# Row maximum over 16384 rows: other load sizes, and other shares of two engines

## The chip, the core and the metric

One core of a Trainium2 chip runs the kernel. The metric is the device time of one execution in microseconds; the median of several runs is compared. Engines: VectorE (DVE) does elementwise work and reductions along a partition's row; ScalarE (ACT) copies; TensorE (PE) transposes here; GpSimd (POOL) can reduce across partitions; SyncE (SP) issues the loads, which 16 DMA engines carry out.

## The reference

```python
def setup_inputs():
    batch, seq, dim = 32, 512, 1024
    return {"x": np.random.randn(batch, seq, dim).astype(np.float32)}

def reference(x):
    return np.max(x, axis=-1).astype(np.float32)
```

So 16384 rows of 1024 numbers, 67.11 MB, are read from memory, and each row gives its maximum.

## The kernel before

**Layout.** The 16384 rows are spread over 128 partitions, 128 rows to each. They come in two blocks of rows: 112 rows a partition, and 16. In each block a partition's rows lie one behind the other in memory, so a load of n rows moves n x 4096 contiguous bytes for each of the 128 partitions. `BLOCKS` lists n for every load, in order. Two rows of the last block are not in the list: they come last, cut at columns 532 and 592 into four `pieces` (`PIECES`), so that little work is left behind the last bytes.

**The ring.** All loads go into `ring`, a buffer of 47 rows a partition behind the results. A load takes the next rows of the ring, or starts again at row 0 if it doesn't fit before its end. `issue()` sends every load as soon as, in the order of the plan, all readers of the rows that it overwrites have been written down; the wait itself is a semaphore on SP. SP issues all loads on one queue in order, so a load that waits holds back all behind it.

**The work on a load.** Load j has n rows. `SHARED[j] = (m, parts)` says that of m of its rows the first `parts` blocks of 128 columns go another way than DVE; the other rows, and what is left of the m, go to DVE. The steps:

- `dj` (direct): DVE takes the maximum of each of the n-m whole rows, one reduce instruction (L78).
- `tk` (turn): for chunk k, at most 8 blocks, PE transposes each block of 128 x 128 into the PSUM tile `ps` (L160), ACT copies this into `sb` (L166), and POOL takes the maximum over all partitions (L168) into `top`. After the transposition the partitions are the columns. `ps`, `sb` and `top` have two buffers each.
- `bk` (back): PE turns each 128 results of chunk k, which lie in one partition's row, into a column (L178), of `got` or of `joint`.
- `pj` (partial): DVE reduces the remaining columns of the m rows to one or more numbers beside these columns, in the same tile.
- `mj` (merge): DVE takes the maximum over blocks and remaining columns of the m rows. Loads named in `RANK` have no merge of their own: their columns stand in one tile, `joint`, and one merge `m99` at the very end takes all of them.
- `fq` (final): DVE reduces one of the four pieces. f2 and f3 take the first result in with them, which stands in the column before their piece.

Before, four loads are shared: three rows of load 10 in full (24 blocks), two rows of loads 13 and 14 by three blocks (6 and 6), and one row of load 17 by two blocks: 38 blocks of 128 columns.

**The order.** `PLAN` is a list of these steps written out by hand, and it is the order of the instructions: `in_turn` ties each instruction to the one ahead of it on the same engine. So every engine works through its instructions in the order of the list, and one that waits for a semaphore holds all behind it. What waits for what follows from the tiles: a reader of a tile waits for its writer, and a writer of a tile or a buffer for those that used it before. Results leave by two stores of ACT: the first block's behind f0, the second block's behind m99.

Of the kernel before, what the change touches and what calls it, by code (L numbers as in the profile page):

```python
# [8 lines left out]
F32 = mybir.dt.float32  # L9

BLOCKS = [
    [2, 15, 16, 14, 11, 11, 10, 10, 8, 8, 7],
    [3, 3, 3, 2, 1, 1, 1],
]
RING = 47


SHARED = {10: (3, 8), 13: (2, 3), 14: (2, 3), 17: (1, 2)}  # L20

RANK = {13: 1, 14: 2, 17: 2}

PIECES = [(532, 492), (592, 432)]

PLAN = """
    d0 d1 d2 d3 d4 d5 d6 d7 d8 d9 t0 d10 t1 t2 d11 b0 d12 b1 d13 t3 p13 b2 p14 t4 m10 d15 b3
    d16 p17 t5 f0 b4 f1 f2 b5 f3 m99
""".split()

NOSYNC = mybir.DependencyInfo(mybir.DependencyClass.NoSync, mybir.DependencyReason.DATA)
# [4 lines left out]
def kernel(  # L41
# [35 lines left out]
    def maximum(out, in_):  # L77
        return in_turn("DVE", nc.vector.reduce_max(out=out, in_=in_, axis=X))  # L78
# [20 lines left out]
    for sizes in BLOCKS:  # L99
# [7 lines left out]
        b, place = 0, {}  # L107
        for i in sorted(range(len(sizes)), key=lambda i: RANK.get(base + i, 0)):
            place[i] = b
# [8 lines left out]
    assert first == I  # L118
    shared = [SHARED.get(j, (0, C)) for j in range(len(loads))]

    lead = [0 if RANK.get(j) == 3 else n - m for j, ((_, n, _, _), (m, _)) in enumerate(zip(loads, shared))]
    final = [j for j in range(len(loads)) if j in RANK]
    final.sort(key=lambda j: loads[j][3])
# [11 lines left out]
    def rows(j):  # L135
        start, n, _, _ = loads[j]
        return ring[:, I + start * D:I + (start + n) * D].rearrange("p (i d) -> p i d", d=D)
# [4 lines left out]
    def share(j):  # L142
        m, parts = shared[j]
        if j in RANK:
            r = loads[j][3] + lead[j] - col0
            return joint[:, r:r + m, :]
        if j not in fetched:
            got = psmall.tile([P, m, parts + (parts < C)], F32)
            fetched[j] = got
        return fetched[j]  # L150
# [39 lines left out]
    def partial(j):  # L190
        m, parts = shared[j]

        s = width - parts if j in RANK else 1
        maximum(share(j)[:, :, parts:], rows(j)[:, lead[j]:lead[j] + m, parts * P:].rearrange(
# [102 lines left out]
```

## Time and profile before

| | |
|---|---|
| median of 3 runs | 163.82 us (163.78 to 163.9) |
| span of the profiled execution | 162.1 us |
| DVE busy | 135.3 us, 83% of the span, 33 instructions |
| POOL busy | 15.9 us, 10 instructions |
| PE busy | 13.6 us, 76 matmuls |
| ACT busy | 6.3 us, 7 instructions |
| moved by DMA | 67.18 MB, mean 414 GB/s |
| mean granted TensorE clock | 0.955 |

The profiled execution has a span of 162.1 us, from its first to its last instruction; the time of a run is taken around that and is 1.7 us longer.

How to read the profile: the span is cut into 40 slices, and a digit is the busy share of an engine in its slice, in tenths. A group of instructions is one line of the code with one form; it shows how often it ran, its busy time, the mean length of one in ns, and the time for which the engine stood idle ahead of it with what ended that. The chain of work that ended last is followed back from the end: at each step to what released the instruction, or to the instruction before it on its engine. In the timeline a line shows start, length, engine, line, operation, and tiles, out<-in; in brackets stands how long the engine was idle, and what released it. For a load, the time from issue to landing is shown. Line numbers are those of the kernel before; in the kernel after they are two less.

### The profile page before, as it was taken

What the parts mean: (1) busy time and instruction counts of PE and PEld (TensorE: products, weight loads), DVE (VectorE), ACT (ScalarE), POOL (GpSimd) and SP (SyncE); (2) the same over time, 40 slices, a digit from 0 to 9 for tenths busy, and PEclk for the clock granted to TensorE, in tenths of its full rate; (3) what the DMA queues carried; (4) which work ended last, traced back from release to release, by engine and by line L of the source; (5) the groups of instructions that cost most, each with busy time, mean ns of one, the idle gap of its engine ahead of it and who ended that gap; (6) DMA issues with size and microseconds to landing.
All of it is one profiled execution on the core that took longest, in us unless ns stands there. A gap on an engine that the chain in (4) does not pass through costs nothing.

```text
span 162.1 us, 295 instructions
## 1 busy us (share of the span) xinstructions
PE 13.6 (8%) x76; PEld 11.7 (7%) x76; DVE 135.3 (83%) x33; ACT 6.3 (4%) x7; POOL 15.9 (10%) x10
## 2 busy tenths in 40 slices
PE   0000000000000000000000000000000000772942
PEld 0000000000000000000000000000000000762731
DVE  3500019998399999999999999996999999999994
ACT  3000000000000000000000000000000000241120
POOL 0000000000000000000000000000000000099791
PEclk9999999999999999999999999999999999996555
DMA  5995999599879999898999799799999989999991
GB/s 178 566 485 258 470 501 517 259 517 517 354 340 439 453 404 534 356 523 367 478 411 475 334 485 475 334 485 388 477 429 388 466 382 446 415 421 416 411 388 34
DMA packets 3456, 67.18 MB, mean 414 GB/s; under 512 B 640, under 2 KB 896, under 8 KB 1536
## 3 DMA queue, kind: packets, MB, share of 16 engines
q1 hardware_dynamic: 3168, 67.11, 96.8%
q10 hardware_dynamic: 288, 0.07, 0.2%
HBM read 67.11 MB, written 0.07 MB: 414 GB/s over the span
## 4 chain that ended last, share of the span: by engine, by line
DMA 50%; DVE 47%; SPq 1%; issue 0%; DVEq 0%
DMA ring<-in_x_dram 50%; DVE ring L78 45%; DVE joint L78 2%; SPq L238 1%; DVEq L292 0%
## 5 line engine op out<-in xcount | busy, mean ns | idle before, releaser
L78 DVE TENSOR_REDUCE ring<-ring 128x1 f32<-128x1024 f32 (+13 forms) x20 | 129.9, 6547 | 23.5 <-DMA ring<-in_x_dram 23.5
L168 POOL PARTITION_ALL_REDUCE top<-sb x6 | 15.7, 2658 | 142.6 <-ACT sb L166 142.5
L160 PE MATMUL ps<-ident,ring 128*128 128x128 f32 x38 | 9.0, 423 | 140.0 <-DMA ring<-in_x_dram 140.0
L160 PEld LDWEIGHTS ps<-ident,ring 128*128 128x128 f32 x38 | 7.6, 225 | 140.1 <-issue 140.1
L166 ACT COPY sb<-ps 128x1024 f32<-128x1024 f32 (+2 forms) x6 | 5.0, 834 | 150.5 <-PE ps L160 143.5
L78 DVE TENSOR_REDUCE joint<-ring 128x2 f32<-128x1280 f32 (+1 forms) x3 | 3.9, 1314 | 0.0
L178 PE MATMUL got<-ident,top 1*128 1x1 f32 x24 | 2.7, 228 | 3.8 <-POOL top L168 3.6
L178 PEld LDWEIGHTS got<-ident,top 1*128 1x128 f32 x24 | 2.4, 188 | 4.6 <-POOL top L168 4.6
L178 PE MATMUL joint<-ident,top 1*128 1x1 f32 x14 | 2.0, 244 | 1.9 <-POOL top L168 1.9
L178 PEld LDWEIGHTS joint<-ident,top 1*128 1x128 f32 x14 | 1.7, 210 | 2.7 <-POOL top L168 2.7
L166 ACT ACT_TABLE_LOAD x1 | 1.3, 1283 | 0.7 <-PEq L281 0.7
L83 DVE MEMSET ident<- 128x128 f32 x1 | 0.2, 165 | 0.8 <-PEq L281 0.8
L90 DVE TENSOR_SCALAR rowno<-rowno 32x1 f32<-32x1 f32 x3 | 0.4, 146 | 0.1
L85 DVE TENSOR_TENSOR_SCAN colno<-ident 128x128 f32<-128x128 f32 x1 | 0.4, 425 | 0.0
L92 DVE TENSOR_SCALAR ident<-colno,rowno 128x128 f32<-128x128 f32 x1 | 0.3, 288 | 0.0
L87 DVE STREAM_TRANSPOSE rowno<-colno 128x32 f32<-128x32 f32 x1 | 0.2, 211 | 0.0
L78 DVE TENSOR_REDUCE ring<-got 128x3 f32<-128x24 f32 x1 | 0.2, 172 | 0.0
L78 DVE TENSOR_REDUCE ring<-joint 128x5 f32<-128x20 f32 x1 | 0.2, 170 | 0.0
L281 POOL MEMSET const-float32-0.0<- 128x1 f32 x1 | 0.1, 98 | 0.2 <-issue 0.2
L281 POOL MEMSET const-bfloat16-1.0<- 128x1 bf16 x1 | 0.1, 102 | 0.0
L281 POOL MEMSET const-uint8-127<- 128x1 uint8 x1 | 0.1, 101 | 0.0
L281 POOL MEMSET const-float32-1.0<- 128x1 f32 x1 | 0.1, 98 | 0.0
(1 smaller groups left out, 0.1 us busy)
## 6 DMA issues: line engine op xcount, KB each, us to landing
ring<-in_x_dram SPq DMA_DIRECT2D x2, 5632.0 KB, 29.9
ring<-in_x_dram SPq DMA_DIRECT2D x2, 5120.0 KB, 36.8
ring<-in_x_dram SPq DMA_DIRECT2D x2, 4096.0 KB, 32.5
ring<-in_x_dram SPq DMA_DIRECT2D x1, 7680.0 KB, 22.6
ring<-in_x_dram SPq DMA_DIRECT2D x1, 7168.0 KB, 58.0
ring<-in_x_dram SPq DMA_DIRECT2D x3, 1536.0 KB, 35.7
ring<-in_x_dram SPq DMA_DIRECT2D x1, 3584.0 KB, 29.2
ring<-in_x_dram SPq DMA_DIRECT2D x2, 1024.0 KB, 17.8
```

Source lines behind the costliest of these rows:

```text
L78: return in_turn("DVE", nc.vector.reduce_max(out=out, in_=in_, axis=X))
L83: in_turn("DVE", nc.vector.memset(ident, 1.0))
L85: in_turn("DVE", nc.vector.tensor_tensor_scan(out=colno, data0=ident, data1=ident, initial=-1.0, op0=ALU.add, op1=ALU.mult))
L87: in_turn("DVE", nc.vector.transpose(out=rowno, in_=colno[:, :32]))
L90: in_turn("DVE", nc.vector.tensor_scalar(out=part, in0=part, scalar1=float(q * 32), scalar2=None, op0=ALU.add))
L92: identity = in_turn("DVE", nc.vector.tensor_scalar(out=ident, in0=colno, scalar1=rowno[:, 0:1], scalar2=None, op0=ALU.is_equal))
L160: in_turn("PE", nc.tensor.transpose(out=ps[:, w:w + P], in_=rows(j)[:, lead[j] + r + i, c * P:(c + 1) * P], identity=ident,))
L166: in_turn("ACT", nc.scalar.copy(out=sb[:, :W], in_=ps[:, :W]))
L168: in_turn("POOL", nc.gpsimd.partition_all_reduce(top[:, :W], sb[:, :W], P, bass_isa.ReduceOp.max))
L178: in_turn("PE", nc.tensor.transpose(out=share(j)[:, r + i, c:c + 1], in_=tops[k][0:1, w:w + P], identity=ident[0:1, 0:1],))
L238: load = nc.sync.dma_start(out=rows(issued), in_=src)
L281: nc = _bacc.Bacc("TRN2", target_bir_lowering=False, num_devices=1)
```

## The change

Only the constants differ; the functions stay as they are.

```diff
 BLOCKS = [
-    [2, 15, 16, 14, 11, 11, 10, 10, 8, 8, 7],
-    [3, 3, 3, 2, 1, 1, 1],
+    [23, 23, 23, 17, 11, 9, 6],
+    [4, 3, 2, 2, 1, 1, 1],
 ]
 RING = 47
-SHARED = {10: (3, 8), 13: (2, 3), 14: (2, 3), 17: (1, 2)}
-RANK = {13: 1, 14: 2, 17: 2}
+SHARED = {0: (3, 8), 1: (4, 8), 2: (6, 8), 3: (5, 8), 4: (11, 1), 5: (9, 2), 6: (1, 8), 7: (4, 2), 8: (1, 4), 9: (1, 4), 10: (2, 1), 11: (1, 4), 13: (1, 2)}
+RANK = {7: 2, 8: 1, 9: 3, 10: 2, 11: 2, 13: 2}
 PIECES = [(532, 492), (592, 432)]
 PLAN = """
-    d0 d1 d2 d3 d4 d5 d6 d7 d8 d9 t0 d10 t1 t2 d11 b0 d12 b1 d13 t3 p13 b2 p14 t4 m10 d15 b3
-    d16 p17 t5 f0 b4 f1 f2 b5 f3 m99
+    d0 t0 t1 t2 b0 b1 b2 m0 d1 t3 t4 t5 t6 b3 b4 b5 b6 m1 d2 t7 t8 t9 t10 b7 t11 b8 t12 b9 b10
+    b11 d3 t13 t14 b12 t15 b13 t16 t17 b14 m2 b15 p4 t18 t19 b16 b17 b18 m3 b19 p5 t20 t21 t22
+    b20 m4 d6 t23 b21 b22 t24 m5 p7 b23 t25 m6 d8 p8 t26 d9 b24 p9 b25 p10 t27 t28 p11 b26 d12
+    b27 p13 t29 f0 b28 f1 f2 b29 f3 m99
 """.split()
```

There are 14 loads in place of 18. The first two take 46 of the ring's 47 rows, and the third starts at row 0 again. Thirteen loads are shared in place of four, with 24, 32, 48, 40, 11, 18, 8, 8, 4, 4, 2, 4 and 2 blocks: 205 in place of 38. Of loads 0 to 3 and 6 whole rows are shared, of loads 4 and 5 all rows by one and two blocks, so that these have no direct reduce. `joint` holds ten rows of six loads in place of five of three. PE has 410 matmuls in place of 76, ACT 30 copies and POOL 30 reductions in place of 6 each, and DVE 28 reduces in place of 25.

## The prediction

> **What bounds the kernel now.** I read the page first, then the granted clock and the queues, then the chain that ended last, and last the end of the timeline. The busy rows of the 40 slices and the queue's own row:
>
> ```profile
> DVE  3500019998399999999999999996999999999994
> DMA  5995999599879999898999799799999989999991
> q1 hardware_dynamic: 3168, 67.11, 96.8%
> ```
>
> Three pieces of the chain that ended last (start, length, what):
>
> ```profile
> 111.01 38.94 DMA ring<-in_x_dram
> 149.97 1.22 DVE ring L78
> ...
> 159.14 0.59 DVE ring L78
> ```
>
> Two things run full. The load queue's packets fill 96.8% of the span on 16 engines: 67.11 MB take from about 1.7 to 158.6 us and nothing is free in between. VectorE (DVE), idle 23.5 us in all in the first 111 us, then works almost without a gap to the end. The chain follows the loads up to 149.95 and DVE from there. Both meet at the end; first the issue of the last piece with its time to landing, then the timeline (start, length, what):
>
> ```profile
> ring<-in_x_dram SPq DMA_DIRECT2D x1, 216.0 KB, 9.0
> ```
>
> ```profile
> 145.33 0.65 PE L178 MATMUL got<-ident,top 1*128 1x1 f32 x8 [1.06 <-POOL top L168]
> ...
> 148.54 1.01 PE L178 MATMUL got<-ident,top 1*128 1x1 f32 x8 [2.56 <-POOL top L168]
> ...
> 150.09 1.51 PE L160 MATMUL ps<-ident,ring 128*128 128x128 f32 x6 [0.54 <-DMA ring<-in_x_dram]
> ...
> 152.58 6.17 POOL L168 PARTITION_ALL_REDUCE top<-sb  x3 [0.89 <-ACT sb L166]
> ...
> 157.28 2.46 DVE L78 TENSOR_REDUCE ring<-ring 128x1 f32<-128x532 f32 x4
> ...
> 159.66 0.17 DVE L78 TENSOR_REDUCE ring<-joint 128x5 f32<-128x20 f32 x1
> ```
>
> The last piece (216 KB, issued at 149.97) is seen landed at 158.97; its reduce f3 starts at 159.14, the last merge m99 at 159.66, and the span ends 2.4 us after that, by the last store and the closing steps. If DVE were infinitely early, f3 could start 0.15 us sooner and no more. So the change can gain only by a shorter load stream; it can lose by anything that makes DVE late after about 150 us.
>
> Prices of DVE, from the forms:
>
> ```profile
> L78 DVE TENSOR_REDUCE ring<-ring 128x16 f32<-128x16384 f32 x1 | 17.2, 17221 | 3.2 <-DMA ring<-in_x_dram 3.2
> ...
> L78 DVE TENSOR_REDUCE ring<-ring 128x1 f32<-128x433 f32 x1 | 0.6, 595 | 0.0
> ```
>
> The slope is (17221-595)/(16384-433) = 1.042 ns an element, the rest 0.144 us. The four pieces last 0.697, 0.758, 0.657 and 0.595 us (2.71 together) in 2.46 us, so a waiting successor starts 0.08 us before its predecessor's end. From start to start an instruction costs 0.062 us and 1.042 ns an element.
>
> **The load stream: nothing gained, by the count of packets.** Before there are 22 load transfers (18 loads, 4 pieces) of one packet per partition: 2816 packets, and 16 semaphore writes each make 3168. After there are 18, but the built program moves each 23-row load as 128x2 runs of 11776 elements and the 17-row load as 128x2 of 8704. That is 4x2+10+4 = 22 packets a partition again. The bytes are equal, so the stream is as long; I price the difference at 0. A row's share of the stream is 1.212 us: the loads 3 to 7 (56 rows) are seen landed between 43.11 and 110.97. From the 17 rows that are there at 23.78 the new loads land, as a reader sees it, at 31.1 (load 0), 58.9, 86.7, 107.4, 120.7, 131.7 (load 5), 138.9, 143.8 and 147.5. Load 9 ends with the 121st row, as load 13 did, at 149.95; from there both kernels cut alike (2, 1, 1, 1, four pieces): 152.4, 153.7, 155.0, 156.3, and the last piece at 158.97.
>
> **The ring.** Loads 0 and 1 fill 46 of 47 rows, so load 2 waits for all readers of load 0. d0 (20 rows, 21.5 us) ends at 52.6, while load 1 occupies the queue until 58.5: 6 us of cover. Load 3 waits for d1, 58.9+20.4 = 79.3, with 7 us of cover. Load 4 waits for d2, 86.7+18.3 = 105.0; the queue runs empty at 106.5 to 106.9. The first transfer of the trace needs 1.0 us from issue to its first packet, so the cover is some 0.5 us on the first engine and less on the last. I take 0 for it; if the cover fails the stream slips by 0 to 0.6 us, and behind load 4 nine loads wait on SP's queue. Load 6 waits for d3 (120.4) and the stream needs it at 131.2.
>
> **DVE and GpSimd up to load 5.** 167 more blocks leave DVE: 167x128x1.042 ns = 22.3 us. It falls into waits: DVE idles till 31.1, then 52.6 to 58.9, 79.4 to 86.7 and 105.0 to 107.4. A reduce of 1024 columns on POOL takes 3.2 us (three in 9.63 us at 142.05; fitted with the row of 768, 768 and 256 columns in 6.17 us, 0.44 us and 2.7 ns a column). Load 3's five rows end on POOL at 126.7, load 4's at 131.3, so no merge m0 to m3 waits. POOL, ACT and PE here lie under DVE and the stream.
>
> **The tail of DVE, without waits on PE.** p5 starts at 131.7 with load 5. Start-to-start costs: p5 (9x768 elements) 7.26, m4 0.09, d6 5.40, m5 0.09, p7 3.26, m6 0.07, d8 2.20, p8 0.60, d9 1.13. So p9 is due at 151.8, p10 at 152.45 with load 10, p13 with load 13 at 156.35, then f0 to f3 as before: m99 at about 159.6. Alone, this equals the 159.66 of before.
>
> **The tail with its waits: the term that decides.** Loads 7 to 13 nearly all share rows now, and all write the one `joint` tile. In the built program each partial reduce on DVE waits for the back transposes on PE planned ahead of it, and these wait for the partial ahead of them (p8, b24, p9, b25, p10; then p11, b26 and p13, b28), although their columns differ. Before there is one short chain with a full-row reduce between. Step by step: load 9 is seen by PE at 150.09 (the row above, for the same 121st row). t26's 4 transposes at 0.214 us (six in 1.51) end their turn at 150.94; b24's 8 take 1.0 us, with 0.05 to each neighbour, so p9 starts at 152.02 in place of 151.78. It ends at 152.70. b25 then needs 0.13 to start and 0.56 for 4 transposes, to 153.39, and p10 starts at 153.44 in place of 152.46. No reduce stands between p9 and p10 that could fill the gap. Behind p10 (2.0 us) come p11 at 155.51 (it waits for p10's end, 0.05), d12 156.10, p13 157.23, f0 158.09, f1 158.71, f2 159.39, f3 159.97 and m99 160.48. That is 0.82 us after 159.66.
>
> GpSimd gives a second chain: t28's reduce may overwrite its buffer only after b26, which waits for p11's end at 156.18: 156.93, +1.83, +1.13, two back transposes, 160.3. It lies 0.1 us under DVE's and keeps a large part of the loss if DVE's stall is shorter.
>
> The back transposes have two prices: 8 in 0.65 us at 145.33, after 24 unbroken transposes, and 8 in 1.01 us from 148.54, when the granted clock was 0.5. With the short price p9 is on time, p10 starts at 153.06 and m99 at 160.10: +0.45. I take the long one, since the tail's bursts are of 2 to 8. [...]
>
> **More code.** PE's transposes grow from 76 to 410, each a load and a matmul. The trace's packet records hold seven instruction packets of 8192 B (0.31 to 0.50 us each), all before the span; later ones would push data aside on a DMA engine. Bounds: 0 if none falls into the stream, 1.2 us if four fall on one engine. I take 0, the end nearest to what the trace shows. [...]
>
> **Sum.** Stream 0, ring 0, tail +0.82, code 0: span 162.1 to 162.9. The median of the runs is 163.82, 1.7 us over the profiled span; with that kept, 164.65 us. Likeliest's own range: 164.2 (short back transposes, +0.45) to 165.0.
>
> **Rivals.**
> 1. The stream breaks: load 4 comes late by up to 0.6 us, or instruction packets hold one engine back by up to 1.2. Every later landing slips, load 9's too, so it adds to the stall: 163.82+0.82+0.6 to 1.2 = 165.2 to 165.8. For it: 0.5 us of cover at most, and five times the transposes. Against: packets were never in one another's way in the trace. It decides from a landing of the last piece past 159.3.
> 2. No change: the waits on PE are shorter than I cost them (p10 waits under 0.3 us), 163.8. For it: without them the sums are equal. Against: b25 can't start before p9 ends, and even the short rows give +0.45.
> 3. Faster, by the start of the stream: the first load's 2 rows are seen only at 5.65 us, 4.9 us after issue, where 2 rows of a running stream take 2.4. If long packets save about 1 us of that, and p10 waits no more than 0.3 us, all ends near 163.3. Against: the start delay is paid per engine, whatever the packet. It decides from load 0 seen before 30.4.
>
> **How the numbers follow.** Forecast 0.68, rival 1 0.15, rival 2 0.12, rival 3 0.05. A measurement here can tell 0.2%, 0.33 us, from no change: slower 0.83, same 0.12, faster 0.05. The range goes from 164.0, inside rival 2, to 165.8, the end of rival 1.
>
> **What would show it.** Load 0's reduce at 31.1, load 5's at 131.7, the last piece landed at 159.0: the stream is as costed. An idle of about 0.25 us before p9 and 0.6 to 0.7 before p10, both released by PE, and f0 to f3 without a wait for loads: the tail is as costed. If DVE waits for loads in the last 3 us, or if p10 starts with its landing at 152.5, I am wrong.

## The result, and the profile after

The changed kernel takes 168.37 us in the median (168.2 to 168.5, 5 runs), the kernel before 163.84 us: 1.0275 times as long, with a 95% interval of 1.0264 to 1.0287. The direction was forecast, the size was not: 4.5 us in place of 0.8.

The same rows of the page as before, for the changed kernel, and the queue that is new in it:

```profile
span 166.5 us, 1068 instructions
...
DVE  3000000599996089999008999589959999999693
...
DMA  5989989899898998989989999988999899999940
...
q1 hardware_dynamic: 3104, 67.11, 94.7%
...
q8 instruction: 3, 0.05, 0.1%
```

DVE has less to do, as meant (113.6 us busy, before 135.3), and it idles more. The load queue moves the same bytes in 3104 packets: 22 for each partition, 2816, and 18x16 semaphore writes. That is the count that the prediction made. But three packets of another kind now go through the same engines: PE's instructions (when they start, PE has begun 192, 455 and 708 of its 820 weight loads and matmuls).

The timeline of the changed kernel, DVE's reduces from load 2 to load 5, and SP's issue of loads 4 and 5 (start, length, what; in brackets the idle time before):

```profile
88.21 18.29 DVE L76 TENSOR_REDUCE ring<-ring 128x17 f32<-128x17408 f32 x1 [8.84 <-DMA ring<-in_x_dram]
...
106.52 0.82 SPq L236 DMA_DIRECT2D ring<-in_x_dram  x2
...
108.83 12.96 DVE L76 TENSOR_REDUCE ring<-ring 128x12 f32<-128x12288 f32 x1 [2.34 <-DMA ring<-in_x_dram]
...
123.58 10.43 DVE L76 TENSOR_REDUCE got<-ring 128x11 f32<-128x9856 f32 x1 [1.68 <-DMA ring<-in_x_dram]
...
134.50 7.36 DVE L76 TENSOR_REDUCE got<-ring 128x9 f32<-128x6912 f32 x1 [0.39 <-DMA ring<-in_x_dram]
```

Loads 0 and 1 were reduced from 31.00 and 58.85, as costed (31.1, 58.9). Load 2 begins 1.5 us late, load 4 2.9 us late. Between the two, SP issues load 4 at 106.52, 0.03 us behind the end of d2. A window of the trace shows what the 16 DMA engines do then (the window and its length; busy times of PE, PEld, DVE, ACT and POOL, each with its instructions; then granted clock, DMA's busy share, GB/s):

```profile
106.90:107.50 0.60, 0.00 (x0) 0.00 (x0) 0.00 (x0) 0.00 (x0) 0.60 (x2) 0.50 0.38 133
```

133 GB/s against some 430 of a full stream (67.11 MB from 1.7 to 158.6 us before): the queue had run dry. The trace's packet records give each load's 16 landings, one for each engine, and what ran on each engine in order. The median engine, the second latest and the latest tell two kinds of delay apart (us):

```
                       load 2                 load 4                 last piece
                 median  2nd   last     median   2nd   last     median  last
changed kernel   86.11  86.25  87.75    121.72 122.13 123.05    160.14 161.64
e1 (d2 cut)      86.09  86.33  87.41    120.06 121.37 121.59    158.64 159.89
kernel before                                                   158.25 158.56
```

In load 2 fifteen engines are on time and one is 1.5 us behind. In load 4 the median engine is 1.66 us late against e1, the run in which load 4 is issued early enough. The three instruction packets of 16384 bytes started at 70.53, 113.31 and 146.35 us and lasted 1.1, 0.96 and 1.03 us; the data packet behind the first took 2.21 us where 1.74 is usual. So one such packet cost its engine 1.3 to 1.5 us. Where no idle time followed, the engine kept this to the end (in e4 below, 1.3 us with each load). The engine of the first packet lost it again at the dry queue: it still had load 3 to move until 108.38 while the others stood idle, went on with load 4 without a gap, and landed it at 121.77, among the others. The second and third packet met two other engines, after the dry queue; these are the latest of load 4 (123.05) and of the last piece (161.64).

The tail of the changed kernel:

```profile
153.22 1.09 PE L158 MATMUL ps<-ident,ring 128*128 128x128 f32 x4 [1.40 <-DMA ring<-in_x_dram]
153.45 1.21 DVE L76 TENSOR_REDUCE ring<-ring 128x1 f32<-128x1024 f32 x1
154.24 1.01 PE L176 MATMUL joint<-ident,top 1*128 1x1 f32 x8
155.28 0.69 DVE L76 TENSOR_REDUCE joint<-ring 128x1 f32<-128x512 f32 x1 [0.62 <-PE joint L176]
...
156.12 0.56 PE L176 MATMUL joint<-ident,top 1*128 1x1 f32 x4 [0.88 <-DVE joint L76]
...
156.72 2.76 DVE L76 TENSOR_REDUCE joint<-ring 128x8 f32<-128x1792 f32 x2 [0.74 <-PE joint L176]
...
163.74 0.20 DVE L76 TENSOR_REDUCE ring<-joint 128x10 f32<-128x50 f32 x1
```

This is the ping-pong that the prediction described: b24 holds p9 for 0.62 us, p9 holds b25, b25 holds p10 for 0.74 us. From p10 to m99 it is 7.02 us, predicted 7.04. All of it stands 3.3 us later than predicted, since it hangs on load 9, which PE saw at 153.22 and not at 150.09.

### The profile page after: what moved, and what is told of

It is laid out like the page before. It is cut to its first block, busy times and chain, and to the rows that moved or that the text cites. A ratio compares the mean times of both kernels' runs of the same rounds, so it can differ in the third digit from the quotient of the medians.

```text
span 166.5 us, 1068 instructions
## 1 busy us (share of the span) xinstructions
PE 65.4 (39%) x410; PEld 58.3 (35%) x410; DVE 113.6 (68%) x36; ACT 27.9 (17%) x31; POOL 83.9 (50%) x34
## 3 DMA queue, kind: packets, MB, share of 16 engines
q1 hardware_dynamic: 3104, 67.11, 94.7%
HBM read 67.11 MB, written 0.07 MB: 403 GB/s over the span
## 4 chain that ended last, share of the span: by engine, by line
DMA 54%; DVE 37%; another core or an unknown queue 4%; PE 2%; issue 2%; SPq 1%; DVEq 0%
DMA ring<-in_x_dram 54%; DVE ring L76 34%; DVE joint L76 3%; PE joint L176 1%; SPq L236 1%; PE ps L158 1%; DVEq L290 0%
## 5 line engine op out<-in xcount | busy, mean ns | idle before, releaser
L166 POOL PARTITION_ALL_REDUCE top<-sb x30 | 83.7, 2854 | 79.0 <-ACT sb L164 76.8
L76 DVE TENSOR_REDUCE ring<-ring 128x1 f32<-128x1024 f32 (+10 forms) x12 | 85.8, 7170 | 45.9 <-DMA ring<-in_x_dram 45.9
L158 PE MATMUL ps<-ident,ring 128*128 128x128 f32 x205 | 43.1, 392 | 62.1 <-DMA ring<-in_x_dram 61.0
L158 PEld LDWEIGHTS ps<-ident,ring 128*128 128x128 f32 x205 | 37.5, 209 | 63.3 <-issue 58.7
L164 ACT COPY sb<-ps 128x1024 f32<-128x1024 f32 (+3 forms) x30 | 26.6, 888 | 132.8 <-PE ps L158 108.7
L176 PE MATMUL got<-ident,top 1*128 1x1 f32 x181 | 19.8, 226 | 32.1 <-POOL top L166 24.6
L176 PEld LDWEIGHTS got<-ident,top 1*128 1x128 f32 x181 | 17.9, 184 | 36.7 <-POOL top L166 30.8
L76 DVE TENSOR_REDUCE got<-ring 128x11 f32<-128x9856 f32 (+1 forms) x2 | 17.8, 8895 | 2.1 <-DMA ring<-in_x_dram 2.1
L76 DVE TENSOR_REDUCE joint<-ring 128x1 f32<-128x512 f32 (+3 forms) x6 | 8.4, 1402 | 1.4 <-PE joint L176 1.4
L76 DVE TENSOR_REDUCE ring<-got 128x3 f32<-128x24 f32 (+6 forms) x7 | 1.3, 179 | 0.0
```

The costliest lines, as they stand in the source:

```text
L158: in_turn("PE", nc.tensor.transpose(out=ps[:, w:w + P], in_=rows(j)[:, lead[j] + r + i, c * P:(c + 1) * P], identity=ident,))
L164: in_turn("ACT", nc.scalar.copy(out=sb[:, :W], in_=ps[:, :W]))
L166: in_turn("POOL", nc.gpsimd.partition_all_reduce(top[:, :W], sb[:, :W], P, bass_isa.ReduceOp.max))
L176: in_turn("PE", nc.tensor.transpose(out=share(j)[:, r + i, c:c + 1], in_=tops[k][0:1, w:w + P], identity=ident[0:1, 0:1],))
```

## The experiments

Theory A: the loss comes from the load stream (an instruction packet makes one engine late, d2 therefore ends late, load 4 meets a dry queue) and a smaller part from the tail. Theory B: the tail's waits are all of it.

**e1: no dry queue.** The direct reduce of load 2 is cut, so that load 4 waits for its first 11 rows only.

```diff
-        maximum(res[:, col + k:col + k + n - m], rows(j)[:, k:k + n - m, :])
+        cut = 11 if j == 2 else n - m
+        for u, v in ((0, cut), (cut, n - m)):
+            if v > u:
+                maximum(res[:, col + k + u:col + k + v], rows(j)[:, k + u:k + v, :])
```

> The changed kernel with the direct reduce of load 2 cut in two, 11 rows and 6, so that load 4, which overwrites only the first 11, needs not wait for the whole. Theory A (the stream: one 16 KiB instruction packet at 70.5 us makes one engine 1.5 us late with load 2, d2 ends 1.5 us late, load 4 is issued when the queue has run dry): load 4 is issued near 100 us, no engine runs dry at 106.9, the median engine's last piece lands about 1.4 us sooner, the time falls by 1.0 to 1.6 us to some 167.0; the late engine keeps its delay. Theory B (the loss is the waiting of DVE for PE in the tail alone): below 0.2 us of change, 168.4.

Measured 166.9 us, 1.0185 [1.017, 1.0201] of the kernel before: 1.5 us faster than the changed kernel. From its timeline: d2 in its two cuts, SP's issue of load 4 and, some 6 us later, of load 5, then p4 and m99:

```profile
87.94 18.35 DVE L76 TENSOR_REDUCE ring<-ring 128x11 f32<-128x11264 f32 x2 [8.48 <-DMA ring<-in_x_dram]
...
99.85 6.85 SPq L239 DMA_DIRECT2D ring<-in_x_dram  x2
...
122.13 10.43 DVE L76 TENSOR_REDUCE got<-ring 128x11 f32<-128x9856 f32 x1 [0.50 <-DMA ring<-in_x_dram]
...
162.00 0.20 DVE L76 TENSOR_REDUCE ring<-joint 128x10 f32<-128x50 f32 x1
```

d2 begins as late as ever, for the late engine is still there; load 4 is issued 6.7 us sooner, all engines go on at their pace, and p4 begins 1.45 us sooner. Theory A holds here, B falls.

**e2: no waits between DVE and PE in `joint`.** The partial maxima of the six loads in `joint` get a tile of their own; a small maximum at the end joins both.

```diff
+    rest = once.tile([P, count], F32)
+    both = once.tile([P, count], F32)
+    in_turn("DVE", nc.vector.memset(joint, -3.0e38))
+    in_turn("DVE", nc.vector.memset(rest, -3.0e38))
...
+        if j in RANK:
+            r = loads[j][3] + lead[j] - col0
+            maximum(rest[:, r:r + m], rows(j)[:, lead[j]:lead[j] + m, parts * P:])
+            return
...
-            maximum(res[:, col0:col0 + count], joint)
+            maximum(both, joint)
+            in_turn("DVE", nc.vector.tensor_tensor(
+                out=res[:, col0:col0 + count], in0=both, in1=rest, op=ALU.max))
```

> The changed kernel with the partial maxima of the joint loads in a tile of their own, so that no partial on DVE waits for a back transpose on PE or the other way round; it adds two memsets at the start and one small maximum at the end. Theory A: the idle of DVE before p9 and p10 (0.62 and 0.74 us) goes, the end is then set by the last piece (seen at about 162.1 us), so 0.7 to 1.2 us are gained, some 167.4. Theory B (the tail's waits are all of it): back to within 1 us of the kernel before, below 165.

Measured 167.78 us, 1.0241 [1.0224, 1.0258]: 0.6 us faster, just under what A expected. Both idle times are gone:

```profile
153.55 1.21 DVE L76 TENSOR_REDUCE ring<-ring 128x1 f32<-128x1024 f32 x1
154.68 0.68 DVE L76 TENSOR_REDUCE rest<-ring 128x1 f32<-128x512 f32 x1
155.62 2.61 DVE L76 TENSOR_REDUCE rest<-ring 128x2 f32<-128x1792 f32 x2 [0.26 <-DMA ring<-in_x_dram]
...
162.79 0.20 DVE L76 TENSOR_REDUCE both<-joint 128x10 f32<-128x50 f32 x1
163.02 0.17 DVE L206 TENSOR_TENSOR ring<-both,rest 128x10 f32<-128x10 f32 x1
```

p10 now waits for its load. The merge of `joint` ends 0.95 us sooner than m99 did, and the extra instruction gives 0.23 us of it back.

**e3: loads 0 and 1 by DVE alone.** This was to remove the first instruction packet; chunks 0 to 6 and m0, m1 leave `PLAN`, and the later chunks are counted anew.

```diff
-SHARED = {0: (3, 8), 1: (4, 8), 2: (6, 8), ...
+SHARED = {2: (6, 8), ...
```

> The changed kernel with loads 0 and 1 reduced by DVE alone (112 PE matmuls fewer: 298). Theory A: the instruction packet at 70.5 us goes with them (PE reaches its 256th instruction only after load 2), load 2 is seen whole at 86.7 us in place of 88.2, d2 ends at 105.0, the queue runs dry for less than 0.5 us, and the time falls by 1.0 to 1.6 us; two instruction packets stay, later. A rival (GpSimd's and PE's work beside the loads slows DMA by itself, by the amount of work): load 2 is as late as before or late by less in proportion, a gain of some 0.5 us at most.

Measured 169.12 us, 1.0326 [1.0306, 1.0346]: slower than the changed kernel, a miss for both theories. The packet at 70.5 us was gone, as expected. But d0 now takes 24.69 us, so that load 2 was issued at 55.88, some 2.1 to 2.7 us before its engines ran out of work at 58.0 to 58.6, and load 3 at 83.74, 2.5 us before the first engine ran out. By the packet records five engines still stood idle for 0.3 to 1.0 us ahead of load 2, the first or second packet of each engine took 2.0 to 2.7 us where 1.74 is usual, and the median engine landed 0.5 us late; load 3's landed 1.2 us late. So an issue 2.1 to 2.7 us before the engines ran out was not enough here. These delays don't explain why the run is slower than the changed kernel, though: load 4's median engine landed at 121.73, as there (121.72). What differs in the profiled run, the slowest of the four (169.67 us), is one engine. It began load 4 as the last, at 109.42, and then had an instruction packet at 114.56 too; it landed load 4 at 124.30 and the last piece at 162.51, against 161.64 for the latest engine of the changed kernel. Two delays on one engine added up here.

**e4 and e7: more code on PE, in the kernel before.** 128, or 384, transposes of the identity at the start, into scratch PSUM, whose results nobody reads:

```diff
+    for g in range(0, 128, 8):
+        ps = psum.tile([P, D], F32)
+        for c in range(8):
+            in_turn("PE", nc.tensor.transpose(
+                out=ps[:, c * P:(c + 1) * P], in_=ident, identity=ident))
```

> The kernel before with 128 more transposes of the identity on PE at the start, into scratch PSUM, whose result nobody reads. Theory A: PE's instructions grow by 256, one 16 KiB instruction packet falls into the stream, one DMA engine is 1.1 to 1.5 us late from there to the end (it was busy all the time and can't catch up), and the time grows by 0.7 to 1.5 us, to about 164.9. The rival (instruction packets cost nothing, they are fetched beside the data): 163.8, within 0.2.

> The kernel before with 384 more transposes of the identity on PE at the start, in place of 128: 768 more instructions, three instruction packets of 16 KiB. If each falls on another DMA engine, the latest engine still carries one delay of 1.3 us: 165.2, as with 128. If all fall on one engine the delays add: 3.5 to 4 us, about 167.5. If the cost were PE's work beside the loads and not the packets, it would be three times that of 128 too, but on all engines alike.

Measured 165.21 us for 128 (1.0083 [1.0068, 1.0098]) and 165.28 us for 384 (1.0079 [1.0061, 1.0097]): 1.4 us each. The queue's row of e4, then two lines of its timeline:

```profile
q8 instruction: 1, 0.02, 0.0%
```

```profile
44.40 66.55 DVE L78 TENSOR_REDUCE ring<-ring 128x16 f32<-128x16384 f32 x5 [3.19 <-DMA ring<-in_x_dram]
...
160.94 0.17 DVE L78 TENSOR_REDUCE ring<-joint 128x5 f32<-128x20 f32 x1
```

The kernel before has in place of the first of these two lines:

```profile
43.13 66.53 DVE L78 TENSOR_REDUCE ring<-ring 128x16 f32<-128x16384 f32 x5 [3.20 <-DMA ring<-in_x_dram]
```

The queue's row of e7:

```profile
q8 instruction: 3, 0.05, 0.1%
```

One packet at 18.60 us, and load 2 is reduced from 44.40, where the kernel before began at 43.13; m99 comes 1.28 us later. Fifteen engines land each load as before, the sixteenth 1.3 us late. So it is not PE's work beside the loads that costs: three times that work (e7) costs the same 1.4 us. With 384 transposes there are three packets (16.37, 30.62 and 44.70 us), and in load 4 three engines are late by one delay each (74.23, 74.29 and 74.44, all others by 72.97). The cost is that of the latest engine: three packets on three engines cost what one did.

**e5: both edits of e1 and e2.**

> The changed kernel with both edits: the direct reduce of load 2 cut in two (alone 1.5 us faster), and the partial maxima in a tile of their own (alone 0.6 us faster). Theory A (the losses lie one behind the other: a dry queue, one late engine, waits in the tail): they add, 166.0 to 166.4, the last piece lands near 160 as with the cut alone, and what is left over the kernel before, about 2.3 us, is the late engine's 1.3 us and the longer end. Rival (the two hide each other): 166.8, no faster than the cut alone.

Measured 166.21 us, 1.014 [1.0121, 1.0158]. They add: 0.7 us below e1. The last piece landed at 160.08 us, 1.5 us later than in the kernel before, by the late engines: its median engine landed at 158.35, within 0.1 us of the kernel before.

**e6: load 4 issued barely ahead of the dry queue, with no late engine before it.** Load 1 goes to DVE alone and is cut at row 17, so that load 3 is not late; the first instruction packet comes at 97.73 us, when load 2 has landed. As in e3, the steps that fall away leave `PLAN` and the later chunks are counted anew.

```diff
-SHARED = {0: (3, 8), 1: (4, 8), 2: (6, 8), ...
+SHARED = {0: (3, 8), 2: (6, 8), ...
...
+        cut = 17 if j == 1 else n - m
```

> The changed kernel with load 1 reduced by DVE alone, in two cuts (17 rows and 6, so that load 3 is issued earlier than before); 64 PE matmuls fewer, so the first instruction packet comes after load 2 has landed, and d2, uncut, ends near 105.0: load 4 is issued about 1.9 us before the queue runs dry, with no late engine ahead of it. Theory A1 (a load that is issued less than some 3 us ahead of a dry queue pays nearly the full restart, as loads 2 and 3 did in the third run): the first packets of load 4 are long by about 1 us, its median engine lands near 121.2. Theory A0 (the prediction's: 1.0 to 1.8 us of cover is enough): load 4's median engine lands near 120.1, no long packets but that of an instruction.

Measured 167.58 us, 1.022 [1.0191, 1.0249]. From its timeline:

```profile
86.87 18.29 DVE L73 TENSOR_REDUCE ring<-ring 128x17 f32<-128x17408 f32 x1 [3.11 <-DMA ring<-in_x_dram]
...
105.18 0.82 SPq L236 DMA_DIRECT2D ring<-in_x_dram  x2
```

That is 0.8 us faster than the changed kernel. Load 4 was issued at 105.18, 1.4 to 1.8 us before its engines were through with load 3 (one, with the instruction packet, later). Its first packets took 1.8 to 2.4 us in place of 1.67 on these, one engine stood idle for 1.5 us, and the median engine landed at 120.48, 0.4 us later than in e1. That lies between the two expectations: the cover is not enough, but falling short by this much costs 0.4 us and not 1.

**e8 and e9: GpSimd's work beside the loads, in the kernel before.** 24 reductions across partitions at the start, each with a memset of its source, whose results nobody reads; in e9 also one copy of a column on ACT ahead of them (the first two lines).

```diff
+    warm = once.tile([P, 1], F32)
+    in_turn("ACT", nc.scalar.copy(out=warm, in_=ident[:, 0:1]))
+    for g in range(24):
+        sb = turned.tile([P, D], F32)
+        in_turn("POOL", nc.gpsimd.memset(sb, 0.0))
+        top = allr.tile([P, D], F32)
+        in_turn("POOL", nc.gpsimd.partition_all_reduce(top, sb, P, bass_isa.ReduceOp.max))
```

> The kernel before with 24 reductions of 1024 columns across partitions on GpSimd at the start, each with a memset of its source, whose results nobody reads: about 80 to 100 us of GpSimd beside the loads and DVE, and no instruction more on PE. Theory A: DMA and DVE keep their pace, 163.8 within 0.2 us. Rival (GpSimd's work beside DVE or the loads slows either): DVE's reduces are longer than their prices, or the loads land later; over 164.2.

> As the run before, 24 reductions of 1024 columns on GpSimd beside the loads in the kernel before, and one small copy on ACT at the start, so that ACT's table is loaded early, as in the kernel before. In the run without that copy the table load (1.28 us) waited for PE's first transposes at 140.9 us, and the chain PE, ACT, GpSimd ended 0.8 us late. Theory A (GpSimd's work costs neither the loads nor DVE anything; the 1.3 us of that run are the table load): 163.9 within 0.25 us. Rival (something else of GpSimd's work costs it): 165 again.

Measured 165.17 us (1.0075 [1.0059, 1.0091]) for e8, a miss for theory A, but not for the rival's reason: loads and DVE kept their pace (the last piece landed at 158.46, the reduce of 16 rows took 17.222 us). The groups show what happened (busy, mean ns, then idle before):

```profile
L166 ACT ACT_TABLE_LOAD x1 | 1.3, 1283 | 140.9 <-PE ps L160 140.9
...
L78 DVE TENSOR_REDUCE ring<-joint 128x5 f32<-128x20 f32 x1 | 0.2, 180 | 0.5 <-PE joint L185 0.5
```

In the built program ACT's first copy now waited for GpSimd too, and the wait for PE went to the table load ahead of it. So the 1.28 us of the load moved from the start to 140.9 us, onto the chain PE, ACT, GpSimd, PE, and m99 waited 0.5 us for b5. With the early copy (e9) 164.22 us are left, 1.0023 [1.0014, 1.0033]: most of the 1.3 us were the table load. The remaining 0.4 us are more than theory A allowed. In the profiled run the loads from 142 us on land 0.15 to 0.3 us later than in the kernel before; why was not settled.

## Why the prediction was wrong

**The sum.** Predicted 164.65, measured 168.37. m99 came at 163.74 where 160.48 was costed: 3.26 us. The rest is the end: 2.74 us from m99 to the end of the span in place of 2.44, and 0.2 us between span and median. PE saw load 9 3.13 us late: by the packet records its median engine landed 1.73 us later than the same 121st row before (150.91 against 149.18), its last engine 1.73 behind the median (152.64) where 0.33 was usual, 1.4 us more. Most of the first part is the dry queue's (in e1, without it, the median engine landed load 9 at 149.38); the second is that of the third instruction packet, on whose engine the latest landing falls. The direction came out as forecast, and the term that it rested on, the tail's waits, was there; but that term is 0.6 to 0.7 of the 4.5 us, and most of the loss comes from the two terms that were put at 0.

**The step on code failed, by its value.** "I take 0, the end nearest to what the trace shows" was the wrong end of the bounds: the trace had no kernel with long code under a full queue, so it could show no such packet. One packet made one engine 1.3 to 1.5 us late (e4, the changed kernel), and three that met different engines cost what one did (e7, 1.4 us). The upper bound, "1.2 us if four fall on one engine", was too small for a single packet: it priced each at some 0.3 us by the packets of 8192 B ahead of the span (the record has six of these, not seven), and under the stream they have 16384 B and take 1.0 to 1.1 us. PE itself shows little of this: in the changed kernel its waits for loads (61.0 us) and for POOL, DVE and ACT (37.1 us together) and its work (65.4 us) leave 3.0 us of the span. The delay shows in the load stream, which uses every engine.

**The step on the ring failed, by its value and by what it left out.** The words "the cover is some 0.5 us on the first engine" took the time from issue to first packet for enough. e6 shows that an issue 1.4 to 1.8 us ahead still cost 0.4 us, and e3 that one 2.1 to 2.7 us ahead cost about 0.5. Issues 5.5 us ahead and more cost nothing measurable (load 2's first packet took 1.74 us, the pace, on every engine; e1's load 4, 6.7 us ahead, landed at 120.06 on its median engine). The price of a queue run dry was bounded at 0.6 us; it was 1.66, some 0.9 of idle engines by the packet records and 0.7 in longer first packets.

**The two are one chain.** Rival 1 named both, joined by "or", and its sign, a last piece past 159.3, was seen (161.64); its sum of 165.2 to 165.8 was still too low, for it priced each of them too small. In the run an instruction packet caused the late load: a late engine in load 2 put off the whole of d2, since the reduce waited for the latest engine (it landed at 87.75, d2 began at 88.21); d2 put off load 4 by 1.5 us; and a cover of 1.5 us was gone. So the first packet was paid by all engines as a dry queue, at which its own engine caught up; the later packets were paid as late engines at the end. Against e6, where no engine was late ahead of d2, load 4's median engine landed 1.24 us later; of its 1.66 us the remaining 0.4 are the short cover itself.

**What held.** The stream's count of packets (2816 before and after), the landings of loads 0 and 1, POOL and PE under cover up to load 5, and the half clock in the tail (a granted clock of 0.50 from 142.98 us on, 8 back transposes in 1.01 us). That short bursts bring that clock was the prediction's assumption; no run shows what sets it. Load 0 was seen at 31.00 and p10 waited 0.74 us, so rivals 3 and 2 fall. At the start the slowest first packet took 0.96 us over the pace with packets of 47104 bytes (2.70 for 1.74 us), much as the 0.91 us before, with 8192 (1.22 for 0.31). The tail's term of 0.82 us was right in kind and about right in size: removing the waits was worth 0.6 us in e2 and 0.7 in e5, and 0.23 us more without the added instruction. p9's wait was larger than costed (0.62 for 0.24) because the late engine of load 9 held t26; p10's was as costed (0.74).

**What the 4.5 us are.** Dry queue 1.5 (e1). Waits in the tail 0.6 to 0.7 (e2, e5). Of the 2.3 us by which e5 still exceeds the kernel before, the last piece's landing gives 1.5, the added instruction 0.2 and the longer way from m99 to the end some 0.3. The remaining 0.25 us lie outside the span: the run is 2.0 us longer than its span, in the kernel before 1.7. Why the end is longer in these two places was not settled. No version of the changed kernel without instruction packets under the stream was made, so that the 1.5 us are theirs is argued from e4 and e7 and from the packet records, not shown by a run without them.

## What to carry to other kernels

Beside a load stream that kept all DMA engines busy, code was a transfer too: in e4, 256 more instructions on PE drew a packet of 16384 bytes through one of them, and the time grew by 1.4 us. Moving work to an engine that needs many small instructions for it can cost more than it relieves (here DVE's busy time fell by 21.7 us and the time grew by 4.5), so count instructions as one counts bytes. Give each load that waits for a buffer a cover of several microseconds, not of one issue time (here 2.1 to 2.7 us were too little and 5.5 us enough), and cut the reader ahead of it, so that it waits only for the rows that it overwrites. Delays on different DMA engines didn't add (e7: 1.4 us for three packets, as for one), two on one engine did (e3: the last piece at 162.51, for 161.64), and a late engine held up the reduce that waited for its whole transfer (d2 of the changed kernel, 1.5 us).

## What was not expected of the hardware

- 128 more transposes on PE, 256 instructions, drew one instruction packet of 16384 bytes and about 1 us through one of the 16 DMA engines that carried data (e4; with 384 in e7 three packets, 14 us apart), and the data packet behind it was longer by 0.3 to 0.5 us (in the changed kernel 2.21 for 1.74, 2.13 for 1.66 and 0.94 for 0.46 us).
- A queue restarted from empty sent first packets that took 1.9 to 2.7 us where 1.67 us is the pace (load 4 of the changed kernel, on the fifteen engines that had run dry); the packet records show no packet of another kind beside them.
- An engine that was late when the queue ran dry was level with the others afterwards (changed kernel, load 4: 121.77 us, the median 121.72).
- The 1.28 us of ACT's table load moved from the idle start to 140.9 us, onto the critical chain, by a wait that GpSimd's work added to the first copy (e8).
